# A hybrid decoder layer on one core: value projection ahead of the LRU input, group norm by half on ScalarE, and seven-product steps in the down projection

## The chip, the core and the metric

The kernel runs on one core of a Trainium2 chip. The engines that matter are TensorE (PE in the profile; PEld is its weight load), VectorE (DVE), ScalarE (ACT), GpSimd (POOL) and SyncE (SP), whose queue issues nearly all transfers. The metric is the device time of one execution in microseconds. Three executions of the kernel before took 1130.82 to 1131.17 us, the median is 1131.03.

## The reference, cut to what is computed

```python
D_MODEL, SEQ, D_FF = 2048, 256, 5632        # float32, batch 1, one layer
u = rmsnorm(h, ln1)
lru_x, lru_g, q, k, v, ret_g = split(u @ W_in, six times 1024 columns)
lru_x = causal_depthwise_conv(lru_x)         # 4 taps
y_lru = rg_lru(lru_x) * gelu(lru_g)          # gates: 8 blocks of 128x128, then a scan over time
y_ret = retention(rope(q), rope(k), v)       # 8 heads of 128, with a decay matrix
y_ret = groupnorm_per_head(y_ret) * silu(ret_g)
h = h + concat(y_lru, y_ret) @ W_out
u = rmsnorm(h, ln2)
h = h + (silu(u @ W_gate) * (u @ W_up)) @ W_down
return rmsnorm(h, final_norm)
```

## The kernel before

**Products.** Every weight is read once as float32 (512 KB a transfer: 128 partitions of 1024 elements, a *raw* tile, 7 buffers). ScalarE rounds it to its high part (`wh`), VectorE subtracts to get the low part (`wl`), four buffers each; the activations are split in the same way. A product is then three matmuls: high times high, high times low, low times high. `Unit` is a weight of two such halves, `split` makes the two parts.

**Order.** All weight steps stand in one list, `program`. For each step the loads of its unit and of three halves more (`AHEAD = 3`) are issued, then its matmuls; `defer(n, f)` puts other work n steps later. Inside that, a scheduler decides the order of instructions on each engine.

**Head.** Group 0 (L788) takes the first 512 columns of the LRU input: for each of the 16 k tiles of x, four blocks of output features times three matmuls of 256 columns, into four PSUM banks. While its weights and x land, `make_u` scales x (ScalarE, L269), takes the low part (VectorE, L270) and feeds the sum of squares: a square on ScalarE (L279) and an addition on GpSimd (L280). `rms_scale` (L242) makes the factor 1/rms; it is applied behind the matmuls, so none of these waits for it. Then for group 0 four chains `lru_in` (scaling, L334; convolution; splitting to `xcs`) and the decay constants (`lru_decay`, a long chain of tiny operations) follow, the four other feature tiles of the LRU input (`fm_tile`, one k tile at a time), and the first gate products (L137, via `lru_gate`).

Then come k and q (8 fm tiles each), v and the retention gate rg (2 blocks of 512 columns each, `tm_block`: tokens as rows, two PSUM banks, 96 matmuls of 512 columns), the retention heads beside rg, the LRU gate lg, and the output projection. `group_norm` (L475 to L489) comes once, two steps behind rg's last block: 16 bn_stats and bn_aggr on VectorE, then on GpSimd 16 tensor_scalar (one a head and token half, L485) and four products with the gate (L489), then transposes `ret_y` (L495).

**FFN.** Eleven blocks `ffn_block` of 512 gate and 512 up columns, eight quads each. A quad is a 2x2 arrangement: two k tiles by gate and up, against two k tiles by two token halves. Its eight block products are made directly, or, for a *summed* quad, as seven products of sums (L611 to L615 sum the weights on VectorE, `Left` the activations). The first two quads of a block are summed. So a block is (2 x 7 + 6 x 8) x 3 = 186 matmuls of 512 columns and 8 transposes (`turn`).

**Down projection.** Four column blocks of 512 through `tm_block` (L148 to L150): 11 units of four k tiles, two token halves, three matmuls each. In the last one, the second token half is cut into two pieces of 256 columns, so that the end (`down_post`: residual, sum of squares, final norm, output) begins earlier. The first block splits `ff` as it goes.

Of the kernel before, what the change touches and what calls it, by code (L numbers as in the profile page):

```python
# [14 lines left out]
P = 128  # L15
D = 2048
S = 256
# [12 lines left out]
SUMMED = 2  # L30
# [3 lines left out]
def tile_hymba_layer(ctx: ExitStack, tc: tile.TileContext, A: dict, out: bass.AP):  # L34
# [8 lines left out]
    tpool = ctx.enter_context(tc.tile_pool(name="tmp", bufs=8))  # L43
    epool = ctx.enter_context(tc.tile_pool(name="conv", bufs=2))
# [9 lines left out]
    def act_tile(name, dt=F32):  # L54
        return apool.tile([P, 512], dt, tag="act", name=nm(name))

# [210 lines left out]
    def make_u(k):  # L267
        hl = act_tile("u", F32R)
        act.activation(out=hl[:, :S], in_=xs(k), func=AF.Copy, scale=col(C_LN1 + k))  # L269
        v.scalar_tensor_tensor(  # L270
            out=hl[:, S:], in0=xs(k), scalar=col(C_LN1 + k), in1=hl[:, :S].bitcast(F32),
            op0=ALU.mult, op1=ALU.subtract,
        )
        u[k] = hl
        if k == 1:
            act.activation(out=sumsq, in_=xt[0], func=AF.Square)
        elif k % 2:
            sq = act_tile("sq")
            act.activation(out=sq, in_=xt[k // 2], func=AF.Square)  # L279
            pool.tensor_tensor(out=sumsq, in0=sumsq, in1=sq, op=ALU.add)  # L280
        if k == KT - 1:
            pool.tensor_tensor(out=sumsq[:, :S], in0=sumsq[:, :S], in1=sumsq[:, S:], op=ALU.add)
# [160 lines left out]
    def head(h):  # L443
# [8 lines left out]
        def pv():  # L452
            c, o = h // 4, (h % 4) * P
            po = aux("pv")
            v0, v1 = vv[c][:, o : o + P], vv[2 + c][:, o : o + P]
            pe.matmul(po[:, 0:P], sc[:, 0:P], v0, start=True, stop=True)
            pe.matmul(po[:, P : 2 * P], sc[:, P : 2 * P], v0, start=True, stop=False)
            pe.matmul(po[:, P : 2 * P], sc[:, 2 * P : 3 * P], v1, start=False, stop=True)
            for t in range(2):
                if oo[2 * t + c] is None:  # L460
                    oo[2 * t + c] = act_tile("o")
                act.copy(out=oo[2 * t + c][:, o : o + P], in_=po[:, t * P : t * P + P])

# [6 lines left out]
    def group_norm():  # L470
        for t in range(2):
            for h in range(NH):
                o = oo[2 * t + h // 4][:, (h % 4) * P : (h % 4) * P + P]
                st = epool.tile([P, 6], F32, tag="st", name=nm("st"))
                v.bn_stats(out=st, in_=o)  # L475
                v.bn_aggr(out=mv[:, 8 * t + h, :], in_=st)
        rsqrt_small(gr, mv[:, :, 1], 1.0, 16)
        v.tensor_scalar(out=gnh, in0=small[:, C_GN : C_GN + NH], scalar1=0.5, scalar2=None, op0=ALU.mult)

    def group_norm_apply(i):  # L480
        t, c = i % 2, i // 2
        for h in range(4 * c, 4 * c + 4):
            o = oo[2 * t + c][:, (h % 4) * P : (h % 4) * P + P]
            n = 8 * t + h
            pool.tensor_scalar(  # L485
                out=o, in0=o, scalar1=mv[:, n, 0:1], scalar2=gr[:, n : n + 1], op0=ALU.subtract, op1=ALU.mult
            )
        o = oo[2 * t + c]
        pool.tensor_tensor(out=o, in0=o, in1=sg[2 * t + c], op=ALU.mult)  # L489
# [45 lines left out]
    def out_post(f, ps):  # L535
# [10 lines left out]
        if f % 2:  # L546
            hh[f // 2] = Left(hf[0], f // 2 < SUMMED)
# [33 lines left out]
    ffh = [None] * (FT // 2)  # L581
    ffl = [None] * (FT // 2)

    class Quad:


        def __init__(self, j, i):
            self.src, self.sums = A["w_gu"][j * (KT // 2) + i], i < SUMMED
            self.parts = {}
# [7 lines left out]
        def load(self, half):  # L597
            r = rpool.tile([P, 1024], F32, tag="raw", name=nm("raw"))
            nc.sync.dma_start(out=r, in_=self.src[:, half * 1024 : half * 1024 + 1024])
            if not self.sums:  # L600
# [27 lines left out]
    def ffn_block(j):  # L628
        quads = [Quad(j, i) for i in range(KT // 2)]
        todo = [(i, p) for i, q in enumerate(quads) for p in (SEVEN if q.sums else EIGHT)]  # L630
        firsts, lasts = {}, {}
        for n, (i, (c, _, _)) in enumerate(todo):
            firsts.setdefault(c, n)
            lasts[c] = n
        ps, at = {}, [0]
        post = ffn_post(j, ps)

        def step(i):
            def run():
                while at[0] < len(todo) and todo[at[0]][0] == i:  # L640
                    n, (c, a, b) = at[0], todo[at[0]][1]
                    if firsts[c] == n:
                        ps[c] = (bank if c[0] == "p" else aux)(c)
                    (ah, al), (bh, bl) = hh[i][a], quads[i].parts[b]
                    pe.matmul(ps[c], ah, bh, start=firsts[c] == n, stop=False)  # L645
                    pe.matmul(ps[c], ah, bl, start=False, stop=False)  # L646
                    pe.matmul(ps[c], al, bh, start=False, stop=lasts[c] == n)  # L647
                    if lasts[c] == n:
                        post(c)
                    at[0] += 1  # L650
                if j == 0 and i == SUMMED:
                    norm2()
                if j == 0 and i > 3:
                    resid_tok(i - 4)
# [3 lines left out]
        for i, q in enumerate(quads):  # L658
            program.append(([q], step(i)))

    def ffn_post(j, ps):
# [21 lines left out]
        def post(c):  # L683
# [15 lines left out]
            if c == "c22":  # L699
                gated(1)  # L700
                defer(3, lambda: turn(0))
                defer(4, lambda: turn(1))

        return post

    def ff_split(p):
        ffh[p], ffl[p] = act_tile("ffh", F32R), act_tile("ffl", F32R)
        split(ffh[p], ffl[p], ff[p])
# [4 lines left out]
    def load_fw():  # L713
        for c in range(4):
            fw[c] = act_tile("fw")
# [7 lines left out]
    def down_post(cb, t, ps, c0, cw):  # L723
        h = htok[(cb, t)][:, c0 : c0 + cw]
        n = cb + (c0 > 0)
        v.tensor_tensor(out=h, in0=ps[:, c0 : c0 + cw], in1=h, op=ALU.add)
# [38 lines left out]
    def load_x(k):  # L765
# [7 lines left out]
    g0 = [  # L773
        Unit(A["w_lx0"][i], 2, lambda k, i=i: load_x(4 * i + k), lambda k, i=i: make_u(4 * i + k)) for i in range(4)
    ]
    g0_ps = []

    def group0(i):
        def run():
            if i == 0:  # L780
                for _ in range(4):
                    g0_ps.append(bank("g0"))
            for k in range(4):
                a = u[4 * i + k]
                for p in range(3):
                    for f in range(4):
                        wh, wl = g0[i].part(k, 512, f * P, P)
                        pe.matmul(  # L788
                            g0_ps[f][:, :S], (wh, wh, wl)[p], a[:, S:] if p == 1 else a[:, :S],
                            start=i == 0 and k == 0 and p == 0, stop=i == 3 and k == 3 and p == 2,  # L790
                        )
                if i == 3 and k == 2:
                    rms_scale(sumsq[:, :S], r1_tok, r1, then)
            if i == 1:
                nc.sync.dma_start(out=ident, in_=A["ident"])
            if i == 3:
                load_gates()
                trig[0] = act_tile("trig")
                nc.sync.dma_start(out=trig[0], in_=A["trig"])

        def then():
            for n in range(4):
                lru_in(n, g0_ps[n])
                defer(5 + n, lambda n=n: lru_gate(n))
            lru_decay()

        return run

    for i in range(4):
        program.append(([g0[i]], group0(i)))  # L810

    for n in range(4, NLRU):

        def post(ps, n=n):
            defer(1, lambda: lru_in(n, ps))
            defer(9, lambda: lru_gate(n))
# [5 lines left out]
        fm_tile(Unit(A["w_lx1"][n - 4]), u, range(KT), post, one=True, room=aux if n < 6 else bank)  # L822
# [16 lines left out]
    for c in range(2):  # L839
        tm_block([Unit(A["w_v"][4 * c + i]) for i in range(4)], lambda k: u[k], lambda t, ps, c0, cw, c=c: v_out(c, t, ps))  # L840

    for c in range(2):

        def post(t, ps, c0, cw, c=c):
            rg_out(c, t, ps)
            if t == 1 and c == 1:
                defer(2, group_norm)
                for i in range(4):
                    defer(2, lambda i=i: group_norm_apply(i))
                for h in range(NH):  # L850
                    defer(7 + h // 4, lambda h=h: ret_y(h))
# [10 lines left out]

    for j in range(NB):
        ffn_block(j)

    for cb in range(4):
        if cb == 0:
            program.append(([], load_fw))
        units = [
            Unit(A["w_down"][11 * cb + i], 1, (lambda k, i=i: ff_split(2 * i + k)) if cb == 0 else None)  # L870
            for i in range(11)
        ]
        tm_block(
            units, lambda k: (ffh[k // 2], ffl[k // 2], (k % 2) * S),
            lambda t, ps, c0, cw, cb=cb: down_post(cb, t, ps, c0, cw),
            together=2 if cb == 3 else 1, split=[(0, 256), (256, 256)] if cb == 3 else (),
        )
# [25 lines left out]
def _tm(w, np):  # L903
# [3 lines left out]
    return a.reshape(n // 512 * (k // 512), P, 2048)  # L907

# [79 lines left out]
```

## Time and profile before

| | us |
|---|---|
| median of three executions | 1131.03 |
| the profiled execution | 1131.17 |
| its span in the trace | 1129.4 |
| TensorE busy in it | 1108.8 |
| VectorE busy | 832.0 |
| ScalarE busy | 590.5 |
| GpSimd busy | 78.7 |

The span is what the trace shows from the first to the last instruction; 1.8 us of the execution lie around it. A row of a timeline gives start, duration, engine, line, operation, out and in, and in brackets the idle time ahead of it with what ended it. A row of groups gives the count, then busy time, mean duration in ns, and the idle time ahead of them. A row of windows gives, behind the stretch, the busy time and the number of instructions of PE, PEld, DVE, ACT and POOL, then the granted TensorE clock, the share of the DMA engines, and GB/s. A duration of a matmul overlaps those of its neighbours.

### The profile page before, as it was taken

The page shows a single profiled execution, that of the slowest core. Times are in us where ns is not written, and L with a number is a line of the kernel's source. Part 1 is how long each engine was busy: PE and PEld are TensorE (multiplying, and loading weights), DVE is VectorE, ACT ScalarE, POOL GpSimd, SP SyncE. Part 2 cuts the span into 40 slices and gives each one's busy share as a digit, 9 for nine tenths or more (in the row PEclk, how much of TensorE's full clock was granted, in tenths as well). Part 3 has the DMA queues.
Part 4 walks back from the last instruction along what each step waited for, and adds up shares of the span by engine and source line. Part 5 has one row for each costly group of instructions (what it writes and reads, how often), then busy time and mean ns, then how long its engine had stood idle before and what let it go on. Part 6 is the DMA issues. An engine that isn't in the chain of part 4 may idle for free.

```text
span 1129.4 us, 15225 instructions
## 1 busy us (share of the span) xinstructions
PE 1108.8 (98%) x5734; PEld 947.9 (84%) x5734; DVE 832.0 (74%) x1115; ACT 590.5 (52%) x780; POOL 78.7 (7%) x82
## 2 busy tenths in 40 slices
PE   8989999999999999999999999999999999999996
PEld 7978888889988988888888888888888888888896
DVE  7698899857867887797797797797795955444544
ACT  7465544456556566554464554554554744343432
POOL 4022220002700000000000000000000000000100
PEclk9989999999999999999999999999999999999998
DMA  8844665645455464664664565655656756666542
GB/s 302 262 140 155 221 203 165 217 159 168 153 184 188 131 242 134 202 220 152 210 221 166 205 211 173 214 192 176 228 178 214 241 188 194 197 189 201 186 151 75
DMA packets 62218, 214.77 MB, mean 190 GB/s; under 512 B 7104, under 2 KB 7488, under 8 KB 62144
## 3 DMA queue, kind: packets, MB, share of 16 engines
q1 hardware_dynamic: 61344, 211.70, 56.9%
q0 software_dynamic: 512, 1.57, 0.4%
q8 instruction: 45, 0.74, 0.3%
q10 hardware_dynamic: 288, 0.52, 0.1%
q14 instruction: 29, 0.24, 0.1%
HBM read 211.67 MB, written 2.10 MB: 189 GB/s over the span
## 4 chain that ended last, share of the span: by engine, by line
PE 93%; POOL 2%; DVE 2%; issue 1%; ACT 1%; DMA 0%; SPq 0%; DVEq 0%; POOLq 0%
PE c L645 12%; PE c L647 12%; PE c L646 12%; PE fm L132 10%; PE tm L149 10%; PE tm L148 10%; PE tm L150 10%; PE fm L133 5%; POOL o L485 2%; PE p L645 2%; PE p L646 2%; PE p L647 2%; PE fm L137 1%; PE fm L138 1%; PE fm L139 1%
## 5 line engine op out<-in xcount | busy, mean ns | idle before, releaser
L94 DVE TENSOR_TENSOR wl<-raw,wh 128x1024 fp32r<-128x1024 f32 (+1 forms) x378 | 453.2, 1209 | 246.5 <-ACT wh L93 242.2
L93 ACT CAST wh<-raw 128x1024 fp32r<-128x1024 f32 (+1 forms) x378 | 386.8, 1033 | 399.5 <-PE tm L150 151.2
L646 PE MATMUL c<-wl,ah 128*128 128x512 f32 x572 | 222.2, 391 | 0.0
L647 PE MATMUL c<-wh,al 128*128 128x512 f32 x572 | 221.3, 389 | 0.0
L645 PE MATMUL c<-wh,ah 128*128 128x512 f32 x572 | 201.3, 390 | 0.3 <-ACT wh L93 0.3
L149 PE MATMUL tm<-wl,ffh 128*128 128x512 f32 (+1 forms) x396 | 144.7, 366 | 0.0
L148 PE MATMUL tm<-wh,ffh 128*128 128x512 f32 (+1 forms) x396 | 144.2, 366 | 0.0
L150 PE MATMUL tm<-wh,ffl 128*128 128x512 f32 (+1 forms) x396 | 144.1, 366 | 0.0
L645 PEld LDWEIGHTS c<-wh,ah 128*128 128x128 f32 x572 | 107.3, 188 | 22.9 <-ACT wh L93 0.5
L646 PEld LDWEIGHTS c<-wl,ah 128*128 128x128 f32 x572 | 107.4, 188 | 22.2 <-DVE wl L94 0.3
L647 PEld LDWEIGHTS c<-wh,al 128*128 128x128 f32 x572 | 107.4, 188 | 22.1
L132 PE MATMUL fm<-u,wh 128*128 128x512 f32 x256 | 93.1, 406 | 0.2 <-DVE xe L334 0.2
L148 PEld LDWEIGHTS tm<-wh,ffh 128*128 128x128 f32 x396 | 74.4, 188 | 12.5
L150 PEld LDWEIGHTS tm<-wh,ffl 128*128 128x128 f32 x396 | 74.3, 188 | 12.1
L149 PEld LDWEIGHTS tm<-wl,ffh 128*128 128x128 f32 x396 | 74.4, 188 | 11.9
L132 PE MATMUL fm<-y,wh 128*128 128x512 f32 x224 | 77.6, 394 | 0.0
L133 PE MATMUL fm<-u,wl 128*128 128x256 f32 x256 | 72.8, 285 | 0.0
L730 POOL TENSOR_TENSOR htok<-htok,fw 128x512 f32<-128x512 f32 (+1 forms) x7 | 9.3, 1323 | 808.0 <-ACT junk L728 808.0
L93 ACT CAST wh<-sum 128x1024 fp32r<-128x1024 f32 x44 | 45.2, 1051 | 36.9 <-PE c L647 24.1
L133 PE MATMUL fm<-y,wl 128*128 128x256 f32 x224 | 61.7, 278 | 0.0
L132 PEld LDWEIGHTS fm<-u,wh 128*128 128x128 f32 x256 | 49.2, 192 | 12.4 <-DVE xe L334 0.5
L137 PE MATMUL fm<-u,wh 128*128 128x256 f32 x192 | 54.8, 286 | 0.0
(232 smaller groups left out, 1642.9 us busy)
## 6 DMA issues: line engine op xcount, KB each, us to landing
raw<-in_w_gu SPq DMA_DIRECT2D x176, 512.0 KB, 4.9
raw<-in_w_down SPq DMA_DIRECT2D x88, 512.0 KB, 4.4
raw<-in_w_out SPq DMA_DIRECT2D x32, 512.0 KB, 3.8
raw<-in_w_k SPq DMA_DIRECT2D x16, 512.0 KB, 4.1
raw<-in_w_q SPq DMA_DIRECT2D x16, 512.0 KB, 3.9
raw<-in_w_v SPq DMA_DIRECT2D x16, 512.0 KB, 3.8
raw<-in_w_rg SPq DMA_DIRECT2D x16, 512.0 KB, 3.8
raw<-in_w_lg SPq DMA_DIRECT2D x16, 512.0 KB, 3.6
```

The lines of the kernel that those rows point to most:

```text
L93: act.copy(out=dst_h, in_=src)
L94: v.tensor_tensor(out=dst_l, in0=src, in1=dst_h.bitcast(F32), op=ALU.subtract)
L132: pe.matmul(ps, wh, hl, start=first, stop=False)
L133: pe.matmul(ps[:, :S], wl, hl[:, :S], start=False, stop=last)
L137: pe.matmul(ps, wh, hl[:, :S], start=first, stop=False)
L148: pe.matmul(ps, ah, wh, start=first, stop=False)
L149: pe.matmul(ps, ah, wl, start=False, stop=False)
L150: pe.matmul(ps, al, wh, start=False, stop=last)
L485: pool.tensor_scalar(out=o, in0=o, scalar1=mv[:, n, 0:1], scalar2=gr[:, n : n + 1], op0=ALU.subtract, op1=ALU.mult)
L645: pe.matmul(ps[c], ah, bh, start=firsts[c] == n, stop=False)
L646: pe.matmul(ps[c], ah, bl, start=False, stop=False)
L647: pe.matmul(ps[c], al, bh, start=False, stop=lasts[c] == n)
```

## The change

It has four parts.

1. The first block of the value projection takes the place of group 0 at the front (`v0`, through `tm_block`). Its output is copied out unscaled and multiplied by 1/rms later, on GpSimd. All eight tiles of the LRU input follow as fm tiles. The squares for the norm come behind `v0`; `rms_scale` is called half-way in the third of these tiles, and its second half in the fourth. The first gates come twelve steps behind their tile.
2. `bn_stats` and `bn_aggr` stand with each head; `group_norm(c)` is called once for each half of the heads, after the rg block that belongs to it. It scales and shifts with 16 ScalarE activations (scale and bias per partition) and multiplies with the gate on VectorE. GpSimd has no part in it.
3. In the FFN, quads 2 and 4 are summed instead of 0 and 1. `raw` has 5 buffers for 7, `act` 58 for 54. The transposed residual (`resid_tok`) is made in blocks 1 and 2; `norm2` stands behind quad 5.
4. The down projection uses quads as the FFN does: two blocks of 1024 columns by 22 pairs of k tiles; pairs 2, 6, 10, 14 and 18 are summed. The two last pairs of a block are one step, ordered by output block, and in the second block only the last output is cut in two halves.

The core of the diff:

```diff
-SUMMED = 2
+SUMMED = (2, 4)
+SUMMED_DOWN = (2, 6, 10, 14, 18)
...
-    apool = ctx.enter_context(tc.tile_pool(name="acts", bufs=54))
+    apool = ctx.enter_context(tc.tile_pool(name="acts", bufs=58))
-    rpool = ctx.enter_context(tc.tile_pool(name="raw", bufs=7))
+    rpool = ctx.enter_context(tc.tile_pool(name="raw", bufs=5))
...
+    def squares():
+        for i in range(KT // 2):
+            sq = act_tile("sq") if i else sumsq
+            act.activation(out=sq, in_=xt[i], func=AF.Square)
+            if i:
+                pool.tensor_tensor(out=sumsq, in0=sumsq, in1=sq, op=ALU.add)
...
-            pool.tensor_scalar(
-                out=o, in0=o, scalar1=mv[:, n, 0:1], scalar2=gr[:, n : n + 1], op0=ALU.subtract, op1=ALU.mult
-            )
-        pool.tensor_tensor(out=o, in0=o, in1=sg[2 * t + c], op=ALU.mult)
+                act.activation(out=oh, in_=oh, func=AF.Identity, scale=gr[:, n : n + 1], bias=gm[:, n : n + 1])
+            v.tensor_tensor(out=o, in0=o, in1=sg[2 * t + c], op=ALU.mult)
...
+    def block(quads, lefts, post, ps, tail=(), after=None):
+        n = len(quads) - (2 if tail else 0)
+        todo = [(i, c, a, b, 0, 512) for i, q in enumerate(quads[:n]) for c, a, b in (SEVEN if q.sums else EIGHT)]
+        for c, c0, cw in tail:
+            todo += [(n, c, a, b, c0, cw, i) for i in range(n, len(quads)) for o, a, b in EIGHT if o == c[:3]]
...
+        quads = [
+            Quad(A["w_down"][d * n + i], i in SUMMED_DOWN, (lambda i=i: make(i)) if d == 0 else None) for i in range(n)
+        ]
+        tail = [("c11", 0, 512), ("c12", 0, 512), ("c21", 0, 512)]
+        tail += [("c22", 0, S), ("c22b", S, S)] if d else [("c22", 0, 512)]
...
+    def then():
+        for t in range(2):
+            pool.tensor_scalar(out=vv[2 * t], in0=vv[2 * t], scalar1=r1_tok[:, t : t + 1], scalar2=None, op0=ALU.mult)
+        defer(2, lru_decay)
...
+    tm_block(v0, lambda k: u[k], v0_out)
+    for n in range(NLRU):
         def post(ps, n=n):
-            defer(1, lambda: lru_in(n, ps))
-            defer(9, lambda: lru_gate(n))
+            defer(max(1, 4 - n), lambda: lru_in(n, ps))
+            defer(max(9, 12 - n), lambda: lru_gate(n))
```

How instructions stand on the engines, at three places. First ScalarE at the head: `wh` is a weight's high part, `u` the scaled x, `sq` a square. Before, within the first k tiles:

```order
L93 CAST wh_144<-raw_143 128x512
L269 ACTIVATE u_151<-x_83,small 128x256
L269 ACTIVATE u_156<-x_83,small 128x256
L279 ACTIVATE sq_159<-x_83 128x512
L93 CAST wh_144<-raw_143 128x512
L93 CAST wh_163<-raw_162 128x512
```

After, where the value block ends (`v` are its copies, `wh_400` a weight of the next tiles):

```order
L101 CAST wh_342<-raw_341 128x1024
L856 COPY v_359<-tm_207 128x512
L856 COPY v_373<-tm_208 128x512
L287 ACTIVATE sq_377<-x_83 128x512
L287 ACTIVATE sq_380<-x_84 128x512
L287 ACTIVATE sq_383<-x_85 128x512
...
L287 ACTIVATE sq_395<-x_89 128x512
L101 CAST wh_400<-raw_399 128x1024
```

The squares have left the k tiles and stand in a row behind the block's two copies, ahead of a weight of the second following tile.

Second GpSimd, behind the last rope products (`n`) and ahead of the final norm (`htok`). Before, with `o` the heads' output:

```order
L423 TENSOR_TENSOR n_1912<-qk_1859,sr 128x256
L485 TENSOR_SCALAR o_2331<-o_2331,mv,gr 128x128 x4
L485 TENSOR_SCALAR o_2333<-o_2333,mv,gr 128x128 x4
L485 TENSOR_SCALAR o_2545<-o_2545,mv,gr 128x128 x4
L485 TENSOR_SCALAR o_2547<-o_2547,mv,gr 128x128 x4
L489 TENSOR_TENSOR o_2331<-o_2331,sg_2471 128x512
L489 TENSOR_TENSOR o_2333<-o_2333,sg_2488 128x512
```

After:

```order
L431 TENSOR_TENSOR n_1946<-qk_1893,sr 128x256
L430 TENSOR_TENSOR m_2064<-qk_2060,sr 128x256
L431 TENSOR_TENSOR n_2065<-qk_2012,sr 128x256
L807 TENSOR_TENSOR htok_4750<-htok_4750,fw_7987 128x512
L807 TENSOR_TENSOR htok_4821<-htok_4821,fw_7989 128x512
```

All rows of the group norm have gone from this engine; nothing stands between rope and the final norm.

Third VectorE at the summed quad 4 of an FFN block after the change (`raw_5933` and `raw_5964` are the quad's two halves, `raw_5890` and `raw_5927` those of the plain quad ahead of it, `sum` the summed weights, `bl` and `wl` low parts):

```order
L619 TENSOR_TENSOR sum_5966<-raw_5933 128x512
L102 TENSOR_TENSOR wl_5893<-raw_5890,wh_5892 128x1024
L620 TENSOR_TENSOR sum_5966<-sum_5966,raw_5964 128x512
L102 TENSOR_TENSOR bl_5936<-raw_5933,bh_5935 128x512
L622 TENSOR_TENSOR sum_5967<-raw_5933,raw_5964 128x512
L623 TENSOR_TENSOR sum_5967<-sum_5966,raw_5964 128x512
L102 TENSOR_TENSOR wl_5930<-raw_5927,wh_5929 128x1024
L102 TENSOR_TENSOR wl_5971<-sum_5966,wh_5970 128x1024
L102 TENSOR_TENSOR wl_5977<-sum_5967,wh_5976 128x1024
```

and before the change, at the first summed quad of a block (`raw_5018` and `raw_5048` its halves, `raw_4976` and `raw_4982` the two of the quad ahead):

```order
L611 TENSOR_TENSOR sum_5050<-raw_5018 128x512
L612 TENSOR_TENSOR sum_5050<-sum_5050,raw_5048 128x512
L94 TENSOR_TENSOR wl_4949<-raw_4946,wh_4948 128x1024
L94 TENSOR_TENSOR wl_4979<-raw_4976,wh_4978 128x1024
L614 TENSOR_TENSOR sum_5051<-raw_5018,raw_5048 128x512
L615 TENSOR_TENSOR sum_5051<-sum_5050,raw_5048 128x512
L94 TENSOR_TENSOR wl_4985<-raw_4982,wh_4984 128x1024
```

In both, sums that need the quad's second half stand ahead of low parts of the quad before; after the change the low part of `raw_5927` is behind all four sums.

More of the change, by code (lines that the diff above doesn't have):

```diff
@@ L599, in load @@
             nc.sync.dma_start(out=r, in_=self.src[:, half * 1024 : half * 1024 + 1024])
+            if half == 0 and self.before:
+                self.before()
             if not self.sums:
@@ L640, in run, with ffn_block, after @@
                 while at[0] < len(todo) and todo[at[0]][0] == i:
[L641 to L648, printed above, removed]
+                    m, (_, c, a, b, c0, cw, *q) = at[0], todo[at[0]]
+                    if firsts[c] == m:
+                        ps[c] = (aux if c in ("c11", "c12", "c21", "c22") else bank)(c)
+                    q = q[0] if q else i
+                    (ah, al), (bh, bl) = lefts[q][a], (t[:, c0 : c0 + cw] for t in quads[q].parts[b])
+                    p, last = ps[c][:, c0 : c0 + cw], lasts[c] == m
+                    pe.matmul(p, ah, bh, start=firsts[c] == m, stop=False)
+                    pe.matmul(p, ah, bl, start=False, stop=False)
+                    pe.matmul(p, al, bh, start=False, stop=last)
+                    if last:
                         post(c)
                     at[0] += 1
[L651 to L654, printed above, removed]
[L656 to L659 removed]
+                if after:
+                    after(i)
+            return run
+        for i in range(n):
+            program.append(([quads[i]], step(i)))
+        if tail:
+            program.append((quads[n:], step(n)))
+    def ffn_block(j):
+        def after(i):
+            if j == 0 and i == SUMMED[-1] + 1:
+                norm2()
+            if j in (1, 2) and i < 2:
+                resid_tok(2 * j - 2 + i)
+            if j == NB - 1 and i == 0:
+                load_fw()
+        ps = {}
+        quads = [Quad(A["w_gu"][j * (KT // 2) + i], i in SUMMED) for i in range(KT // 2)]
+        block(quads, hh, ffn_post(j, ps), ps, after=after)
     def ffn_post(j, ps):
@@ L809, in tile_hymba_layer, with v0_out @@
-    for i in range(4):
-        program.append(([g0[i]], group0(i)))
-    for n in range(4, NLRU):
+    v0 = [
+        Unit(A["w_v"][i], 2, lambda k, i=i: load_x(4 * i + k), lambda k, i=i: make_u(4 * i + k)) for i in range(4)
+    ]
+    def v0_out(t, ps, c0, cw):
+        vv[2 * t] = act_tile("v")
+        act.copy(out=vv[2 * t], in_=ps)
+        if t == 0:
+            return
+        nc.sync.dma_start(out=ident, in_=A["ident"])
+        squares()
+        defer(2, load_gates)
+        defer(3, lambda: halfway.append(lambda: rms_scale(sumsq[:, :S], r1_tok, r1, then)))
@@ L861, in tile_hymba_layer, with swap @@
         fm_tile(Unit(A["w_out"][f]), y, order, lambda ps, f=f: out_post(f, ps), one=f >= KT - 2)
+    def swap():
+        early.close()
+        late.append(ctx.enter_context(tc.tile_pool(name="late", bufs=5)))
+    program.append(([], swap))
     for j in range(NB):
         ffn_block(j)
[L866 to L877, printed above, removed]
+    for d in range(2):
+        down_block(d)
     AHEAD = 3
```

177 lines of the change are left out of this document (89 added, 88 removed).

## The prediction

> **What bounds the kernel now.** I read first the page's head with its first part (busy time by engine), then the chain of work that ended last, then the waits of TensorE.
>
> ```profile
> span 1129.4 us, 15225 instructions
> PE 1108.8 (98%) x5734; PEld 947.9 (84%) x5734; DVE 832.0 (74%) x1115; ACT 590.5 (52%) x780; POOL 78.7 (7%) x82
> ...
> PE 93%; POOL 2%; DVE 2%; issue 1%; ACT 1%; DMA 0%; SPq 0%; DVEq 0%; POOLq 0%
> ```
>
> TensorE (PE) is busy for all but 1129.4 - 1108.8 = 20.6 us, and 93% of the chain is its matmuls. So time can be won in two ways only: fewer or cheaper matmuls, or a share of those 20.6 us. The list of TensorE's waits says where the waits lie:
>
> ```profile
> PE gate L137 <- ACT xcs L93: 4.0, 1, 4.0
> PE g L788 <- DVE u L270: 3.2, 4, 1.0
> PE yt L495 <- POOL o L489: 1.6, 1, 1.6
> PE g L788 <- ACT u L269: 1.1, 2, 0.7
> ...
> PE c L645 <- ACT wh L93: 0.3, 1, 0.3
> PE p L645 <- ACT bh L93: 0.3, 1, 0.3
> ```
>
> Columns: total us, times, longest. The waits are the first LRU gate (4.0), the first projection (3.2 + 1.1), the group norm (1.6) and the start of the FFN (0.3 + 0.3). What is left of the 20.6 us is the load before the first matmul and the output after the last one:
>
> ```profile
> 1120.42 0.28 PE L150 MATMUL tm<-wh,ffl 128*128 128x256 f32 x1
> ```
>
> That is 1129.4 - 1120.7 = 8.7 us of tail. The price of a matmul is read from the timeline, from start to start (durations of one overlap):
>
> ```profile
> 519.75 0.39 PE L646 MATMUL c<-wl,ah 128*128 128x512 f32 x1
> ...
> 520.43 0.39 PE L646 MATMUL c<-wl,ah 128*128 128x512 f32 x1
> ```
>
> Three steps lie between these rows, so a 512-wide one costs 0.68 / 3 = 0.227 us. A 256-wide one costs 0.12 (five steps between the first two rows of the next fence).
>
> **Step 1a: the first gate.**
>
> ```profile
> 58.04 0.28 PE L137 MATMUL fm<-u,wh 128*128 128x256 f32 x1
> ...
> 58.64 0.28 PE L139 MATMUL fm<-u,wl 128*128 128x256 f32 x1
> 62.94 0.58 PE L137 MATMUL gate<-xcs,gh 128*128 128x256 f32 x1 [4.02 <-ACT xcs L93]
> 63.70 0.80 PE L132 MATMUL fm<-u,wh 128*128 128x512 f32 x1 [0.18 <-DVE xe L334]
> ...
> 68.92 0.39 PE L132 MATMUL fm<-u,wh 128*128 128x512 f32 x1
> ...
> 69.98 0.40 PE L132 MATMUL fm<-u,wh 128*128 128x512 f32 x1
> ...
> 65.00:70.00 5.00, 5.00 (x21) 4.29 (x20) 4.94 (x14) 2.84 (x5) 0.20 (x2) 0.62 0.00 0
> ```
>
> TensorE stands 4.02 + 0.18 us, and then runs slow: from 63.70 to 68.92 it issues eight pairs (a 512 and a 256) in 5.22 us, while from 68.92 to 69.98 three pairs take 1.06, or 0.353 each. Eight would be 2.8, so 2.4 us are lost to the clock, which the windows (last row, the column ahead of the DMA share) give as granted at 0.62. Sum 6.6 us. The changed kernel queues the four `lru_in` chains one step (an fm tile) apart from the scaling and puts four lx and four k tiles, over 40 us of matmuls, between them and the first gate, so I take all 6.6. Ends: 6.6 and, should the clock drop come back in another place, 4.2.
>
> [...]
>
> **Step 1b: value projection in place of group 0.**
>
> ```profile
> 5.44 1.50 PE L788 MATMUL g<-u,wh 128*128 128x256 f32 x8 [0.75 <-ACT u L269]
> ...
> 7.74 1.26 PE L788 MATMUL g<-u,wh 128*128 128x256 f32 x8 [0.32 <-ACT u L269]
> ...
> 9.47 1.37 PE L788 MATMUL g<-u,wh 128*128 128x256 f32 x8
> ...
> 34.86 0.50 PE L242 MATMUL rms<-ones,sumsq 128*128 128x2 f32 x4
> ...
> L93 ACT CAST wh<-raw 128x512 fp32r<-128x512 f32 x16 | 9.2, 612 | 2.5 <-DMA raw<-in_w_lx 2.5
> L269 ACT ACTIVATE u<-x,small 128x256 fp32r<-128x256 f32 x16 | 7.4, 502 | 0.8 <-DMA x<-in_x 0.8
> L279 ACT ACTIVATE sq<-x 128x512 f32<-128x512 f32 x7 | 4.3, 617 | 0.0
> L94 DVE TENSOR_TENSOR wl<-raw,wh 128x512 fp32r<-128x512 f32 x16 | 11.5, 726 | 0.9 <-ACT wh L93 0.8
> L270 DVE SCALAR_TENSOR_TENSOR u<-x,small,u 128x256 fp32r<-128x256 f32 x16 | 9.6, 633 | 0.5 <-ACT u L269 0.5
> ```
>
> Group 0 holds 192 matmuls of 0.12 = 22.9 us but takes 34.86 - 5.44 = 29.4: 6.5 us too long. For each of the 16 k tiles ScalarE needs 0.61 + 0.50 and half of a 0.62 square = 1.42 us, VectorE 0.73 + 0.63 = 1.36 with its operations stretched, against 12 x 0.12 = 1.43 of TensorE: three engines at the same pace, so each stumble stays. The value projection asks 6 x 0.227 = 1.36 of TensorE; ScalarE falls to 1.11 since the squares come afterwards. The first tiles still wait for x: k = 1 not before 7.74 (0.94 late after 1.36 for k = 0), k = 2 not before 9.47 (0.37 more). Then 1.3 of the 6.5 us remain and **5.2 come back**. Ends: 6.5 (no wait) and 0 (VectorE at 1.36 paces it as before). I lean to the upper, since VectorE's mean is raised by GpSimd's additions, which leave this stretch.
>
> The 16 x 6 = 96 matmuls moved to the front (21.8 us) are gone from the later value block, and the 192 of group 0 are issued as lx tiles; nothing else in TensorE's sum changes. The squares (8 of 0.62 on ScalarE) and additions (on GpSimd) now lie beside lx 0 to 2, where a tile asks 48 x 0.12 = 5.7 us and needs one weight pair split: cover enough.
>
> **Step 2: group norm off GpSimd.**
>
> ```profile
> 275.17 20.85 POOL L485 TENSOR_SCALAR o<-o,mv,gr 128x128 f32<-128x128 f32 x16 [107.73 <-DVE gr L236]
> 295.99 6.38 POOL L489 TENSOR_TENSOR o<-o,sg 128x512 f32<-128x512 f32 x4
> ...
> 285.36 0.42 DVE L385 SCALAR_TENSOR_TENSOR q<-q,g 128x256 f32<-128x256 f32 x1
> ...
> 295.73 1.23 DVE L94 TENSOR_TENSOR wl<-raw,wh 128x1024 fp32r<-128x1024 f32 x1 [0.22 <-ACT wh L93]
> 296.88 1.48 DVE L385 SCALAR_TENSOR_TENSOR q<-q,g 128x256 f32<-128x256 f32 x1
> ...
> L439 ACT ACT_TABLE_LOAD x1 | 1.3, 1283 | 0.0
> ```
>
> 27 us of GpSimd vanish, but TensorE waited only 1.6 for them: **1.6 us**. In their place ScalarE gets 16 activations of 128x128 (at most the 0.50 of the 128x256 row each, 8 us, in two groups) and VectorE four multiplications (0.69); the program has two more table loads, 1.28 each. The first half's work now has the second rg block's end and the first lg tiles beside it, and ScalarE is about half free. Ends: 1.6 won, and 2.6 lost if both loads fall on a wait.
>
> The rows also price GpSimd's neighbourhood: a weight split beside the tensor_scalar takes 1.23 as everywhere, a 128x256 operation takes 0.42 beside it too (at 285.36), but 1.48 beside the tensor_tensor (at 296.88). [...]
>
> **Step 3: FFN.** The matmuls are as many (two of eight quads summed), their quads now the third and fifth. The two 0.3 us waits at its start fall away with the sums: **0.6 us**. What it may cost is buffers, raw 7 to 5:
>
> ```profile
> raw<-in_w_gu SPq DMA_DIRECT2D x176, 512.0 KB, 4.9
> ...
> L94 DVE TENSOR_TENSOR wl<-raw,wh 128x1024 fp32r<-128x1024 f32 x362 | 441.7, 1230 | 245.6 <-ACT wh L93 241.4 <-PE fm L133 2.6
> L612 DVE TENSOR_TENSOR sum<-sum,raw 128x512 f32<-128x512 f32 x22 | 15.2, 689 | 0.9 <-DMA raw<-in_w_gu 0.5
> ...
> 600.00:700.00 100.00, 100.00 (x451) 82.75 (x450) 81.23 (x94) 51.29 (x58) 0.00 (x0) 1.00 0.55 184
> 900.00:1000.00 100.00, 100.00 (x443) 82.81 (x442) 51.22 (x47) 44.08 (x49) 4.06 (x3) 1.00 0.61 192
> ```
>
> A raw tile lives 4.9 (landing) + about 1.1 (cast) + 1.2 (low part) = 7.2 us, a sum tile about 3 x 0.69 + 2.3 = 4.4. A block of 186 x 0.227 + 1 = 43.1 us uses 16 and 4 of them: 133 tile-us of 5 x 43.1 = 215, 62% full. That is room on average; in a summed quad four of five slots are held at once. I take 0 lost, and the upper end in the rivals.
>
> **Step 4: down projection.** Before, 1056 products of 512 columns, 132 of them cut in two: 924 x 0.227 + 264 x 0.12 = 241.4 us. Now 17 pairs with eight and 5 with seven products, three matmuls each, two blocks: 2 x (136 + 35) x 3 = 1026, of which 12 are cut: 1014 x 0.227 + 24 x 0.12 = 233.1. **8.3 us** less. VectorE is asked more: it was busy 51 us of 100 (window from 900), so half free. In the first block a summed pair needs four weight sums, bl, al, sl (7 x 0.69), three splits (3 x 1.23) and four 128x128 sums, some 9.6 us, against 21 x 0.227 = 4.8 of TensorE; three plain pairs need 3 x (2 x 1.23 + 0.69) = 9.5 against 16.3. Together 19.1 of 21.1: it fits only because loads run three halves ahead. The tail's step of two pairs needs both pairs' halves at its start; I set 0.7 us for the two blocks' ends, and 0.5 for the transposes moved to blocks 1 and 2. The output tail I take as the same 8.7.
>
> **The sum.** The profiled execution took 1131.17 us (span 1129.4 and 1.8 around it; median 1131.03). -6.6 - 5.2 - 1.6 - 0.6 - 8.3 + 0.7 + 0.5 = -21.1: **1110.1 us.**
>
> **Rivals.**
> - *VectorE paces the summed pairs of the down projection.* The surplus of a summed pair is 9.6 - 4.8 = 4.8 us in the first block and 2.4 in the second (no lefts to split). If the lookahead hides half of it, 5 x 2.4 + 5 x 1.2 = 18 us stay, if three quarters, 9. For it: operations in order, sum chains that wait for a landing with splits behind them. Against: the FFN is at 81 of 100 us with the same sums and TensorE has no gap. Time 1119 (up to 1128).
> - *Raw slots stall the FFN too (slower).* The next quad's second half can be fetched only when one of the four held slots comes free. If that is when TensorE starts the summed quad, the half needs 7.2 us against 4.8: 2.4 us stall. There are 22 such quads and ten more below. From (21.1 / 32 =) 0.66 us each the gain is gone; at 1.2 us each 38 come on: 1149. For it: in the row order of VectorE a sum that waits for a landing stands ahead of the split of the quad before. Against: 62% use, and stalls of this size must appear in every summed quad.
> - *The change doesn't do what it says at the front*: the value projection is paced by VectorE or loads, and the 5.2 us stay. Time 1115.3.
>
> **How the numbers follow.** Forecast (1105 to 1113): 0.55. Front not gained: 0.10. VectorE in the down projection, or small stalls in the FFN, between 1113 and 1128: 0.24. Slots, over 1133.3: 0.08. Within 0.2% of before (2.3 us either way; about what a measurement can tell from no change): 0.03. The range 1105 to 1124 leaves out the last two and the far part of the third. Faster is 0.55 + 0.10 + 0.24 = 0.89.
>
> **What would show it.** Right: no wait of TensorE over 1 us after 10 us, the clock at 1.00 from 60 to 70, the value block done near 28.5, TensorE busy some 8 us less in the down projection, FFN blocks 43.1 us apart. Wrong: waits on wl, sum or raw that recur once in a summed quad (rivals one and two: in the down blocks, or in the FFN also), or a v block that ends past 32 us (three).

## The result, and the profile after

The changed kernel takes 1113.05 us (median, 1112.63 to 1113.83) against 1131.08 of the kernel before in the same comparison: a ratio of 0.9842, 95% interval 0.9825 to 0.9859. That is 18.0 us less; the forecast was 1110.1 us, 21 less, with a range of 1105 to 1124. The time fell into the range, 3 us above the forecast and just past 1113, the upper edge of the band to which the forecast gave 0.55. The band above that edge stood for VectorE in the down projection or for small stalls in the FFN, and the profile shows neither.

The page's first part and chain of the changed kernel, in the columns of before:

```profile
span 1110.9 us, 15099 instructions
PE 1096.1 (99%) x5584; PEld 934.2 (84%) x5584; DVE 878.0 (79%) x1229; ACT 617.3 (56%) x826; POOL 58.1 (5%) x64
...
PE 97%; ACT 1%; POOL 1%; DVE 0%; DMA 0%; issue 0%; SPq 0%; DVEq 0%; POOLq 0%
```

All of TensorE's waits (total, times, longest; `warm` is a warm-up ahead of the first product, with the same wait in both kernels), then windows that answer to those of before:

```profile
PE warm L94 <- DVE eps_t L87: 1.0, 1, 1.0
PE tm L156 <- ACT u L277: 0.8, 2, 0.5
PE rms L250 <- POOL sumsq L290: 0.7, 1, 0.7
...
60.00:70.00 10.00, 10.00 (x85) 10.00 (x85) 9.96 (x21) 6.43 (x11) 0.30 (x3) 1.00 0.60 185
398.00:870.00 472.00, 472.00 (x2139) 390.62 (x2138) 375.03 (x447) 251.07 (x283) 0.00 (x0) 1.00 0.58 193
870.00:985.00 115.00, 115.00 (x512) 94.92 (x511) 97.41 (x128) 68.76 (x85) 2.56 (x2) 1.00 0.62 201
```

The gate's and the group norm's waits are gone, and the clock is at 1.00 from 60 to 70. In the FFN (second window) and in the first down block (third) TensorE has no gap at all, although VectorE is busy 97.4 of 115 us there. So neither rival with a busy VectorE or too few raw buffers came about. The front went as walked: the value block's last matmul starts at 28.14, against the 28.5 forecast.

What is missing lies at the other end. The last matmul before began at 1120.42 of 1129.4; now, from the timeline (the first three rows are the last 512-wide matmuls, which close three output blocks):

```profile
1095.56 0.40 PE L660 MATMUL c<-wh,al 128*128 128x512 f32 x1
...
1096.02 0.40 PE L660 MATMUL c<-wh,al 128*128 128x512 f32 x1
...
1096.48 0.39 PE L660 MATMUL c<-wh,al 128*128 128x512 f32 x1
...
1098.38 0.28 PE L660 MATMUL c22b<-wh,al 128*128 128x256 f32 x1
...
1095.99 1.89 DVE L790 TENSOR_TENSOR htok<-c,htok 128x512 f32<-128x512 f32 x3 [5.34 <-PE c L660]
...
1096.71 0.63 ACT L805 ACTIVATE junk<-htok 128x512 f32<-128x512 f32 x1 [7.95 <-DVE htok L790]
...
1098.07 1.28 ACT L809 ACT_TABLE_LOAD   x1
1099.36 0.20 ACT L809 ACTIVATE warm<-ssq 128x1 f32<-128x1 f32 x1
1099.47 0.61 ACT L805 ACTIVATE junk<-htok 128x512 f32<-128x512 f32 x1
...
1101.19 0.29 ACT L817 ACTIVATE r<-ssq,pre 128x1 f32<-128x1 f32 x1
```

Up to the last matmul the kernel won 1120.42 - 1098.38 = 22.0 us, a little more than the 21.1 of the sum. The FFN's first product starts at 386.9 instead of 399.6, so 12.7 us were won ahead of it (forecast 6.6 + 5.2 + 1.6 = 13.4) and 9.3 from there on (forecast 0.6 + 8.3 - 0.7 - 0.5 = 7.7). Behind the last matmul lie now 1110.9 - 1098.4 = 12.5 us instead of 9.0 (counted from its start): 3.5 us were given back. The rows say how. The program writes the last step by output block, c11, c12, c21, c22, so that each is finished while the next is computed. But the three 512-wide outputs close within 0.9 us of each other, and VectorE gets the first only at 1095.99, and then three at once: the scheduler had mixed their matmuls. ScalarE's squares queue up for all three, with the table load for the square root (asked for behind the first of them) in their midst. In spans the miss is 1110.9 - 1108.3 = 2.6 us: 3.5 lost at the end, less the 0.9 won beyond the sum. What the median misses beyond that lies outside the span.

### The profile page after: what moved, and what is told of

Read it like the earlier page. It is cut to its first block, busy times and chain, and to the rows that moved or that the text cites. A ratio compares the mean times of both kernels' runs of the same rounds, so it can differ in the third digit from the quotient of the medians.

```text
span 1110.9 us, 15099 instructions
## 1 busy us (share of the span) xinstructions
PE 1096.1 (99%) x5584; PEld 934.2 (84%) x5584; DVE 878.0 (79%) x1229; ACT 617.3 (56%) x826; POOL 58.1 (5%) x64
## 4 chain that ended last, share of the span: by engine, by line
PE 97%; ACT 1%; POOL 1%; DVE 0%; DMA 0%; issue 0%; SPq 0%; DVEq 0%; POOLq 0%
PE c L658 18%; PE c L659 18%; PE c L660 18%; PE fm L140 10%; PE fm L141 5%; PE fm L146 3%; PE fm L147 3%; PE fm L145 3%; PE p L660 3%; PE p L658 3%; PE p L659 3%; PE tm L156 3%; PE tm L157 3%; PE tm L158 3%; PE ft L705 1%; POOL sumsq L289 1%
## 5 line engine op out<-in xcount | busy, mean ns | idle before, releaser
L659 PE MATMUL c<-wl,ah 128*128 128x512 f32 x864 | 333.1, 391 | 0.0
L660 PE MATMUL c<-wh,al 128*128 128x512 f32 x864 | 331.8, 389 | 0.0
L658 PE MATMUL c<-wh,ah 128*128 128x512 f32 x864 | 292.1, 389 | 0.0
L659 PEld LDWEIGHTS c<-wl,ah 128*128 128x128 f32 x864 | 162.2, 188 | 33.5 <-DVE wl L102 0.4
L658 PEld LDWEIGHTS c<-wh,ah 128*128 128x128 f32 x864 | 162.1, 188 | 33.4
L660 PEld LDWEIGHTS c<-wh,al 128*128 128x128 f32 x864 | 162.3, 188 | 33.0
L102 DVE TENSOR_TENSOR wl<-sum,wh 128x1024 fp32r<-128x1024 f32 x64 | 76.7, 1217 | 2.2 <-ACT wh L101 1.6
L146 PE MATMUL fm<-u,wh 128*128 128x256 f32 x256 | 72.7, 284 | 0.0
L145 PE MATMUL fm<-u,wh 128*128 128x256 f32 x256 | 72.7, 284 | 0.0
L147 PE MATMUL fm<-u,wl 128*128 128x256 f32 x256 | 72.3, 283 | 0.0
L141 PE MATMUL fm<-u,wl 128*128 128x256 f32 x256 | 71.9, 281 | 0.0
L140 PEld LDWEIGHTS fm<-u,wh 128*128 128x128 f32 x256 | 48.1, 188 | 11.7
L146 PEld LDWEIGHTS fm<-u,wh 128*128 128x128 f32 x256 | 49.1, 192 | 0.1
```

Source lines behind the costliest of these rows:

```text
L102: v.tensor_tensor(out=dst_l, in0=src, in1=dst_h.bitcast(F32), op=ALU.subtract)
L140: pe.matmul(ps, wh, hl, start=first, stop=False)
L141: pe.matmul(ps[:, :S], wl, hl[:, :S], start=False, stop=last)
L145: pe.matmul(ps, wh, hl[:, :S], start=first, stop=False)
L146: pe.matmul(ps, wh, hl[:, S:], start=False, stop=False)
L147: pe.matmul(ps, wl, hl[:, :S], start=False, stop=last)
```

## The experiments

Each kernel was compared with the kernel before on the same chip; spans are of one profiled execution each.

**Late gates.** On the kernel before: does the first gate make the stop near 59 us?

```diff
-                defer(5 + n, lambda n=n: lru_gate(n))
+                defer(9 + n, lambda n=n: lru_gate(n))
...
+            tc.keep_in_program_order(pe.matmul(p, wh, xcs[n][:, :S], start=True, stop=False))
```

> The kernel before, with the first four LRU gates nine steps behind their input instead of five, and their first matmul held in program order; nothing else. The prediction's theory (the first gate's wait for xcs is what stops TensorE near 59 us): the stop and the half-clock stretch go, 6.6 us less than before, about 1124.5 us. Rival (the next tile, k 0, has no PSUM bank before lru_in has read group 0's third one, which VectorE does at 63.2 us): TensorE stops in the same place, now on fm <- DVE xe, for 4 to 4.7 us, and the time stays within 1 us of 1131.

Measured: 1130.96 us against 1131.32, ratio 0.9998 (0.9988 to 1.0007). From the waits and timelines of this run, and, as the last row, that of the kernel before that frees the bank:

```profile
PE fm L132 <- ACT xcs L93: 4.9, 1, 4.9
...
62.75 0.74 DVE L334 TENSOR_TENSOR xe<-g,r 128x256 f32<-128x256 f32 x2
...
63.30 0.68 PE L132 MATMUL fm<-u,wh 128*128 128x512 f32 x1 [4.93 <-ACT xcs L93]
...
63.24 0.74 DVE L334 TENSOR_TENSOR xe<-g,r 128x256 f32<-128x256 f32 x2
```

The gate is out of the way and the stop is as long; now k 0 itself stands there. It starts when VectorE has read group 0's third bank (62.75, first of two in that row). The view still names ScalarE's xcs, which k 0 doesn't read; that the bank is what k 0 needed shows in the two runs that follow.

**Late gates and banks**, as above, and

```diff
-        fm_tile(Unit(A["w_lx1"][n - 4]), u, range(KT), post, one=True, room=aux if n < 6 else bank)
+        fm_tile(Unit(A["w_lx1"][n - 4]), u, range(KT), post, one=True, room=aux)
```

> As the run with late gates, and the last two lx tiles take their PSUM banks from the other pool (as the changed kernel does), so that k 0 finds a bank that was read at 43.7 us. Both theories: no stop near 59 us, half-clock stretch gone, 6.6 us less than before, about 1124.5. If the bank is the cause, only this run and not the one with late gates alone shows it; if the gate is, both show the same time. If neither: the stop moves to a later tile.

Measured: 1124.25 us, ratio 0.9937 (0.9922 to 0.9952), 7.1 us less; no wait in that place. **Banks alone**, only the second diff:

> The kernel before, with the last two lx tiles' PSUM banks taken from the other pool, and nothing else: the gates keep their five steps. Theory (the missing bank of k 0 alone makes the stop; the gate is issued ahead of k 0 only because k 0 can't start): TensorE goes on with k 0 at 58.6, the gate follows some 15 us later, no stop, 6.6 us less than before (about 1124.6). Rival (the gate's wait for xcs is a second cause of its own): the stop stays near 4 us, at the gate, and the time at 1129 to 1131.

Measured: 1124.47 us against 1130.96, ratio 0.9941 (0.9928 to 0.9955), 6.5 us less. The timeline, from the last lx matmul to k 0:

```profile
59.35 0.28 PE L139 MATMUL fm<-u,wl 128*128 128x256 f32 x1
59.48 0.40 PE L132 MATMUL fm<-u,wh 128*128 128x512 f32 x1
```

No gap, and the first gate, its five steps unchanged, is issued at 75.0. The bank alone makes the stop; the gate stood ahead of k 0 in TensorE's order only because k 0 had no room to start.

**Group 0 at the front** of the changed kernel, its `v0` taken out (banks and late gates kept, as above):

```diff
-    tm_block(v0, lambda k: u[k], v0_out)
-    for n in range(NLRU):
+    for i in range(4):
+        program.append(([g0[i]], group0(i)))
+    for n in range(4, NLRU):
```

> The changed kernel with group 0 (first half of the LRU input, with the squares beside it) at the front again and the value projection in its old place; the last lx tiles have their banks from the other pool and the gates come late, so that the stop near 59 us doesn't return. The prediction's term for the front: 5.2 us more than the changed kernel (about 1118.2), the last matmul of group 0 near 34.9 us. Rival (the front was bound by loads, and the value projection only moved the wait): under 2 us.

Measured: 1117.87 us, 4.8 more than the changed kernel, but from 1116.26 to 1119.78 in four executions. Its profiled execution is a long one (span 1118.0, group 0's end at 37.44); all of TensorE's longer waits in it are in group 0 (waits first, then two rows of its timeline):

```profile
PE g L868 <- DVE u L278: 4.1, 4, 1.6
PE g L868 <- ACT u L277: 1.6, 2, 1.1
...
29.64 1.48 PE L868 MATMUL g<-u,wh 128*128 128x256 f32 x6
...
31.68 1.12 PE L868 MATMUL g<-u,wh 128*128 128x256 f32 x8
```

In this execution TensorE ran slow too, until 31.68, though none of these waits is longer than 1.6 us: six matmuls take 30.93 - 29.64 = 1.29 us from start to start, 0.215 each instead of 0.12. The ten from 29.64 on take 31.68 - 29.64 = 2.04 us instead of 1.2, so at least 0.8 us were lost.

So the size fits 5.2 us, with some 2 us to either side. The run undoes two things together, the value block and the later squares, and only its slowest execution has a trace: it doesn't tell which of the two gave the time. That the others were shorter for want of such a slow stretch is possible, not shown.

What the traces show is VectorE at its limit. In the kernel before (a window, then the decay constants' operations, with count, busy time and mean in ns):

```profile
25.00:30.00 5.00, 3.97 (x33) 3.77 (x33) 5.00 (x11) 2.02 (x3) 2.07 (x2) 1.00 0.49 157
...
L325 DVE SCALAR_TENSOR_TENSOR lam<-lam,lam 128x8 f32<-128x8 f32 x8 | 5.6, 703 | 0.0
```

VectorE is busy all of the time from 15 to 35 us there (20.00 of 20), while ScalarE has room from 25 on (2.02 of 5 us busy in the window above). The eight operations on `lam` are not in the prediction's 1.36 us a tile. In the changed kernel, where the additions come later, each of them takes 0.17 us instead of 0.70, and a low part of x 0.48 instead of 0.69 (both between 5 and 28 us). So VectorE, with operations that long beside GpSimd's additions, fits as the pace of group 0 better than three engines at one pace; moving the squares alone was not tried.

**Group norm on GpSimd** in the changed kernel, as before, once for all heads:

```diff
-                act.activation(out=oh, in_=oh, func=AF.Identity, scale=gr[:, n : n + 1], bias=gm[:, n : n + 1])
-            v.tensor_tensor(out=o, in0=o, in1=sg[2 * t + c], op=ALU.mult)
+            pool.tensor_scalar(
+                out=o, in0=o, scalar1=mv[:, n, 0:1], scalar2=gr[:, n : n + 1], op0=ALU.subtract, op1=ALU.mult
+            )
+        pool.tensor_tensor(out=o, in0=o, in1=sg[2 * t + c], op=ALU.mult)
```

> The changed kernel with the group norm as before: once, for all heads, scaled and multiplied on GpSimd. The prediction's term: TensorE's wait for it (yt <- o, 1.6 us) is back, about 1.6 us more than the changed kernel. Rival (the two table loads and the sixteen activations on ScalarE cost as much elsewhere): within 0.5 us of the changed kernel.

Measured: 1118.93 us, 5.9 more, over three times the term. And the other way round, **the new group norm in the kernel before**:

> The kernel before, with the group norm of the changed one (by half, on ScalarE and VectorE) and nothing else. The prediction's term: 1.6 us less than before (about 1129.6), no wait of TensorE on yt. Rival (undoing the norm in the changed kernel cost 5.9 us, so the term is worth 5 us wherever it stands): about 1126. The size in either kernel depends, by the first theory, only on how late GpSimd is for TensorE there: 1.6 us in the one, 3.9 us and a clock drop in the other.

Measured: 1130.01 us against 1130.96, ratio 0.9991 (0.9982 to 1.0000): about 1 us less. The wait on yt is gone there, 1.6 us. For the size in the changed kernel, its waits, GpSimd's timeline and a window:

```profile
PE yt L503 <- POOL o L497: 3.9, 1, 3.9
...
277.11 23.05 POOL L493 TENSOR_SCALAR o<-o,mv,gr 128x128 f32<-128x128 f32 x16 [98.81 <-ACT q L394]
300.14 4.97 POOL L497 TENSOR_TENSOR o<-o,sg 128x512 f32<-128x512 f32 x4
...
300.00:320.00 20.00, 18.27 (x99) 15.96 (x100) 9.94 (x17) 9.71 (x19) 5.11 (x5) 0.91 0.37 112
```

The same work on GpSimd took 28.0 us here and 27.2 before (23.05 against 20.85 up to the first product with the gate), TensorE reached the transposes a little sooner after its start, and the wait grew from 1.6 to 3.9. Behind it the clock drops (0.91 over 20 us), which the wait of 1.6 before the change didn't bring (1.00 from 296 to 305). In the profiled execution the last matmul starts 1103.75 - 1098.38 = 5.4 us later: 3.9 are the wait, an estimated 1.2 the slow stretch behind it (half of the 2.35 us shown in the last section), and the front ended 0.5 later here, which need not be the norm's doing. Whether the longer GpSimd time is a matter of neighbours or of chance was not tried.

**No summed pair in the down projection** (`SUMMED_DOWN = ()`) in the changed kernel:

> The changed kernel with no summed pair in the down projection (all 22 pairs with eight products). If TensorE alone sets the pace there (as the prediction's sum has it): 30 matmuls of 512 columns come back, 30 x 0.227 = 6.8 us, and since the end can change too with another order of the last matmuls, 5 to 9 us more than the changed kernel (about 1119.9). Rival (VectorE's sums cost something that the busy TensorE hides): the difference is under 5 us. VectorE's busy time falls by about 45 us in the down projection under both.

Measured: 1118.08 us, 5.0 more. Last matmul and the window of the first down block:

```profile
1105.01 0.28 PE L660 MATMUL c22b<-wh,al 128*128 128x256 f32 x1
...
870.00:985.00 115.00, 115.00 (x512) 95.09 (x511) 63.40 (x65) 54.73 (x68) 0.48 (x1) 1.00 0.59 197
```

The last matmul starts 1105.01 - 1098.38 = 6.6 us later: 30 x 0.227 = 6.8 holds. The rest of the difference is the end, which is 1.1 us shorter in this kernel (1116.4 - 1105.0 = 11.4). VectorE does 34 us less in the window (57.6 less in the whole kernel, 820.4 against 878.0, more than the 45 expected), and TensorE's gain shows no sign of it. The rival, VectorE as the pace, falls.

**Four raw buffers** (`bufs=4`) in the changed kernel:

> The changed kernel with four raw buffers instead of five. By the slot theory of the prediction's second rival, a summed quad then holds all four, and nothing of the next quad can be fetched before one comes free: 32 summed quads with a stall of 1 to 3 us each, 30 to 90 us more. If slots are not what holds this kernel (a block needs 133 tile-us of 4 x 43.1 = 172, 77% full), under 5 us. Either shows how far five buffers stand from the point where they cost.

Measured: 1114.89 us, 1.8 more. Two waits on weights show, of 0.4 and 0.6 us, both in the first down block (at 936 and 943 us); in the FFN's window TensorE is busy all 472 us as with five. The last matmul starts at 1100.74, 2.4 us later than with five, so more is lost than these waits. The slot theory with its 30 to 90 us is refuted, and for five buffers more clearly.

**The end: square root early.** In the changed kernel:

```diff
-            if (cb, t) == (2, 0):
+            if (cb, t) == (1, 1):
                 act.activation(out=warm, in_=ssq[:, t, n : n + 1], func=AF.Sqrt)
```

> The changed kernel, with the table load for the final square root called for at the end of the first down block (at column block 1, token half 1) instead of behind the first output of the last step. Theory (ScalarE's chain of squares with the table load of 1.28 us between them sets the end): the span ends 1.3 to 1.5 us earlier than the changed kernel's 1110.9, TensorE's part is the same. Rival (the end is set by the output transfers or by VectorE, not by ScalarE): under 0.4 us.

Measured: 1111.3 us, ratio to before 0.9825 (0.9808 to 0.9841), span 1109.1: 1.8 us less in both. Its last matmul:

```profile
1098.12 0.28 PE L660 MATMUL c22b<-wh,al 128*128 128x256 f32 x1
```

Behind it lie 11.0 us instead of 12.5, so 1.5 are the table load's; the other 0.3 come ahead of it. **The end: outputs in order**, the last step's three matmuls each held in place:

```diff
+                    mm = tc.keep_in_program_order if tail and i == n and "c22b" in lasts else (lambda x: x)
-                    pe.matmul(p, ah, bh, start=firsts[c] == m, stop=False)
+                    mm(pe.matmul(p, ah, bh, start=firsts[c] == m, stop=False))
```

> The changed kernel, with the matmuls of the very last step held in the order the program writes: all of c11, then c12, c21, and the two halves of c22. Theory (the end grew from 8.7 to 12.2 us because three outputs finish within 0.7 us of each other): c11 is ready about 8 us and c12 about 5.5 us ahead of the last matmul, the end behind the last matmul shrinks to about 8.7, the span to about 1107.4; up to 1 us is given back if TensorE has to wait for low parts. Rival (the end is long since the last half has only 12 matmuls and GpSimd's products queue): it stays above 11 us.

Measured: 1111.01 us, ratio 0.9822 (0.9807 to 0.9836), span 1108.8. TensorE's new wait, its last matmul, and VectorE's and ScalarE's first rows of the end:

```profile
PE c L660 <- DVE wl L102: 0.8, 1, 0.8
...
1099.64 0.28 PE L661 MATMUL c22b<-wh,al 128*128 128x256 f32 x1
...
1091.62 0.69 DVE L791 TENSOR_TENSOR htok<-c,htok 128x512 f32<-128x512 f32 x1 [0.82 <-PE c L661]
...
1093.09 1.28 ACT L810 ACT_TABLE_LOAD   x1
```

The first block is added at 1091.62 instead of 1095.99, the table load lies beside matmuls, and behind the start of the last matmul there are 1108.8 - 1099.6 = 9.2 us, as before the change (9.0). So the mixing was the cause of the 3.5 us. Of these, 0.8 went back into a wait for a low part, and the front ended 0.4 us later in this execution.

**Both at the end** (here another way of holding: only the first matmul of each output behind c11 is held, and in the last steps of both down blocks):

> The changed kernel with both changes at its end: the table load for the square root at the end of the first down block, and the last step's outputs held in order (c11, c12, c21, both halves of c22). If the two are one cause (the squares and the load come together behind the last matmuls), the second adds nothing to the first: the span is that of the run with ordered outputs, 1108.8 +- 0.4. If they are two costs, it is 1.5 us shorter still, 1107.3.

Measured: 1112.11 us, span 1109.8, longer than either. The last matmul starts at 1100.60, so behind it again 9.2 us: with the outputs in order the early load adds nothing that shows, though the edit differs from the ordered run's in more than the load. But TensorE waits 2.0 us for low parts in three places, two of them at the first block's end, where the order was free before. The expected span missed those.

**Pair 17 instead of 18 summed**, with the outputs of the last step in order:

> The run with ordered outputs, and the last summed pair of the down projection is pair 17 instead of 18, so that VectorE's seven operations on its parts are over before the low parts of the last step. Theory (TensorE's one wait of 0.76 us in the last step is for a low part queued behind those operations): the wait goes, the span is 1108.0 instead of 1108.8. Rival (the low part is late because its buffer is freed late by TensorE itself): the wait stays and the span is 1108.8 +- 0.3. Either way the end behind the last matmul stays at 8.9 us.

Measured: 1110.61 us against 1131.29, ratio 0.9816 (0.9803 to 0.9829), the fastest here. The wait is gone from the view, which fits a low part queued behind VectorE's operations, and not the rival. The span is 1109.2, though, not 1108.0: the front ended 0.8 us later than in the run it is compared with (first gate at 100.1 against 99.3), and from there to the last matmul's start the two are 999.9 and 1000.3 us, only 0.4 apart. That it is faster than the ordered run alone (1111.01) is therefore not shown.

## Why the prediction was right, point by point

- **Step 1a, the stop near 59 us**: size right (6.6 forecast, 6.5 with the banks alone), cause wrong. The prediction took the row's releaser, the first gate waiting for xcs, and argued from the gate's later place. The late gate gained nothing by itself. What removes the stop in the kernel before is other banks for the last lx tiles. The changed kernel has them too, as `room=aux if n in (2, 3, 6, 7)` in its full diff, and the prediction gave that no term. That the time came out is luck: the change moved the bank along with the gate. Whether the stop would return in the changed kernel with the old banks was not tried. The row below the gate's in the prediction's own fence, `fm` with `DVE xe L334` as releaser, was the hint: xe is what empties the bank. The slow stretch behind the stop (granted clock 0.50 from 64 to 68 us) counted as the prediction said: 2.4 us by it, and 6.5 less the 4.2 of the stop are 2.3.
- **Step 1b, the value block**: 5.2 forecast, 4.8 by undoing it, with a wide spread; its end at 28.4 against 28.5. Of the bounds, 0 and 6.5, the reason for leaning up (GpSimd's additions leave the stretch) fits the shorter VectorE operations there (0.48 us for a low part of x instead of 0.69); "three engines at the same pace" fits less well, since VectorE alone was full to the end of group 0.
- **Step 2, the group norm**: 1.6 forecast; about 1 alone, at the edge of what the interval can tell from nothing, and 5.9 with the rest of the change. A wait is no constant of its step: it is the difference of two arrivals, and the other parts moved them.
- **Step 3, FFN**: as forecast, no gap, the 0.6 us gone; five buffers are enough, and four cost 1.8 us.
- **Step 4, down projection**: as forecast. 6.6 of the 6.8 us of the products left out are seen at the last matmul, and VectorE's 9.6 us for a summed pair don't show at TensorE (34 us more in a window of five summed pairs is 6.8 a pair above a plain one; the forecast has 9.6 - 3.15 = 6.5). That it is the loads running ahead that hide them is argued, not tried. The two allowances, 0.7 for the blocks' ends and 0.5 for the transposes, had no row behind them, and no run shows them: FFN and down projection together won 9.3 instead of 7.7.
- **The failed term**: "The output tail I take as the same 8.7." It grew by 3.5 us, more than the whole miss of 3.0. I read the order of the tail in the program, where each output closes in turn, and not the order of its instructions on TensorE, where they close together. Two experiments show it: order alone brings the tail back to its old length, and moving the table load takes 1.5 us of it (1109.1 - 1098.1 = 11.0 instead of 12.5).
- **Two readings of the hardware.** On the clock: stops of 3.9 us (granted 0.91 over the 20 us around it), 4.0 (0.50 from 64 to 68) and 4.9 (0.82 from 65 to 70) came with a slow stretch, and the one of 1.6 in the kernel before didn't (1.00 from 296 to 305); but with group 0 at the front, where none was longer than 1.6 us, TensorE ran slow too (0.215 us a matmul instead of 0.12). So here no single length of a stop tells the two cases apart. On GpSimd beside VectorE: the changed kernel's timelines of GpSimd and VectorE at the squares and the v scalings, and last a split of the kernel before:

```profile
29.80 12.57 POOL L289 TENSOR_TENSOR sumsq<-sumsq,sq 128x512 f32<-128x512 f32 x7 [28.94 <-ACT sq L287]
...
48.49 3.42 POOL L866 TENSOR_SCALAR v<-v,r_tok 128x512 f32<-128x512 f32 x2 [4.45 <-DVE r_tok L244]
...
33.81 5.71 DVE L102 TENSOR_TENSOR wl<-raw,wh 128x1024 fp32r<-128x1024 f32 x3 [4.98 <-ACT wh L101]
...
49.27 1.21 DVE L102 TENSOR_TENSOR wl<-raw,wh 128x1024 fp32r<-128x1024 f32 x1
...
284.21 1.23 DVE L94 TENSOR_TENSOR wl<-raw,wh 128x1024 fp32r<-128x1024 f32 x1 [0.25 <-ACT wh L93]
```

Beside the additions (a tensor_tensor) three splits take 5.71 us, 1.9 each instead of 1.23; beside the scaling (a tensor_scalar, 1.71 each) one takes 1.21. The prediction's own row for a split beside the tensor_scalar, at 295.73, in fact lies beside the tensor_tensor from 295.99 on; the row at 284.21 lies wholly beside the tensor_scalar and takes 1.23 as well, so the reading stands. By these rows, as in the prediction, of these two only the tensor_tensor goes with longer VectorE operations, though not with every one: the split at 295.73 took 1.23 beside it. The one wait of TensorE near the additions is the 0.7 us for the sum of squares.

## What to carry to other kernels

Read a wait as a list of everything that the waiting work needs, buffers and banks too, and look at the next row: the named releaser was not the cause of the 4.0 us here, and a change that moves two things at once can prove a wrong reason right. When a step is written to end output by output, check the instruction order on the engine, since a scheduler may let them end together, and then all that follows queues up at the only place where nothing covers it. A wait's price is the difference of two arrivals; it changes with every other edit, and a stop can cost clock on top: those of 3.9, 4.0 and 4.9 us did here, the one of 1.6 us in the kernel before didn't, and with group 0 at the front TensorE ran slow behind waits of at most 1.6 us.

## What was not expected of the hardware

The slow stretch behind a stop differed in length, and in one run its start lagged. Behind 4.0 us it lasted from 63.70 to 68.92 (5.2 us; a pair of matmuls took 0.64 us at 64.51 and 0.35 from 68.92 on). In the run with late gates, behind 4.9 us, from 63.30 to 66.56 (3.3 us). Behind the 3.9 us in the run with the norm on GpSimd, TensorE first went on at full pace for 2 us (from 301.45) and was slow from 303.52 to 305.87 only:

```profile
302.06 0.40 PE L140 MATMUL fm<-y,wh 128*128 128x512 f32 x1
302.30 0.28 PE L141 MATMUL fm<-y,wl 128*128 128x256 f32 x1
302.42 0.40 PE L140 MATMUL fm<-y,wh 128*128 128x512 f32 x1
...
304.31 0.63 PE L140 MATMUL fm<-y,wh 128*128 128x512 f32 x1
304.74 0.41 PE L141 MATMUL fm<-y,wl 128*128 128x256 f32 x1
304.95 0.63 PE L140 MATMUL fm<-y,wh 128*128 128x512 f32 x1
```

The pair takes 0.36 us at 302 and 0.64 at 304. So the price of these stops of 3.9 to 4.9 us was each itself, and an estimated 1.2 to 2.4 us more, by the length of the slow stretches. With group 0 at the front, where no wait was longer than 1.6 us, a slow stretch cost at least 0.8 us as well.
